# Head pairs on halves of the matmul array, and the 32-blocks of a delta rule's inverse computed on GpSimd

## The chip, the core and the metric

One core of a Trainium2 chip. The metric is the device time of one launch in microseconds. The kernel before took 853.67 us (median of 3 runs, 853.37 to 853.96). In the profile PE is the matmul engine TensorE, PEld its weight loads, DVE VectorE, ACT ScalarE, POOL GpSimd and SP SyncE, whose queue carries the weight loads from memory.

## The reference, cut to what matters

Two transformer-like blocks on 256 positions of width 1024, all float32. The first block has a state-space mixer (SSM, 16 heads of 64 columns, which the kernel computes as one causal 256 x 256 product per head), a gated linear recurrence, two gates and a feed-forward part. The second block has four branches of width 512: a gated delta rule (4 heads), a spatial gating, a sliding-window attention (8 query heads of 64, 2 key heads) and an attention over a memory (4 heads), each gated, projected up and summed.

The delta rule needs, for each chunk, the solution of a unit lower triangular system:

```
L = where(strict, (kb @ k^T) * exp(diff), 0)
sol = triangular_solve(eye + L, rhs, lower, unit_diagonal)
u, w = sol[..., :dv], sol[..., dv:]
v_new = u - w @ S;  o = qg @ S + a_qk @ v_new;  S = S * d + kd^T @ v_new
```

The reference works in chunks of 64; the kernel uses two chunks of 128 for each of 4 heads, which is the same function. So there are eight matrices of 128 x 128 to invert.

## The kernel before

The projections make up most of the work. Each weight chunk of 256 columns (or 512) is loaded by SP's queue as two tiles `wraw` of 128 x 1024, split by ACT (`whi`, L112) and DVE (`wlo`, L113) into two rounded parts, and multiplied with the activations `HH` and `HL` in three float32r matmuls per 128 rows (`mm3`, L397 to L399). A float32 matmul that is not of this kind appears as two instructions in the trace.

The order of PE's instructions is the order in which the program is written (`tc.manual_schedule` for the tensor engine). The class `Weave` writes it: the main generator (`block1`, then `block2`) emits projections and yields once after every 12 matmuls of 256 columns or 6 of 512, which is one tick. Side generators do the rest of the work; a side yields a number of ticks to wait or an event and ticks after it, and at each tick at most two sides (in block 2) take a step, in the order in which they were added: `decay`, `delta`, `memory`, `window`, `spatial`. When the main generator yields a side's name, that side is run to its end at that point (a join). The other engines' instructions are ordered by the framework.

The SSM side (`side_ssd`) makes for each head a decayed 256 x 256 matrix `M` and multiplies it with that head's 64 columns (`head`, L656 and L658). The columns stand in `XD`, for each head a 128-wide tile of which the other 64 columns are zero, so that two heads of a pair are added up into one bank `py`.

The window side (`side_window`) has for each of 8 heads a step of scores (a mask, L1326, and two products with the keys, L1327 and L1329), a step of transposes (`turn`, L1358) and a step of values (L1370, L1372). The heads of a pair lie on the two halves of the partitions; `SK` and `SV` hold keys and values with the other half zero, so that each product runs over the whole array.

The delta side (`side_delta`) computes `LT` (the transpose of L, L1144), then the inverse by doubling: level 0 on DVE (L1155, L1156) and a transpose (`pi`, L1161), then levels 1 to 6. A level l merges blocks of 2^l into blocks of 2^(l+1): a product `pit` (L1177) of 64 columns per head, a multiplication by a mask (L1180), from level 2 on a transpose `piy` of the inverse so far (L1187), a product `pix` (L1197) and an addition (L1204). Level 6 works on 64 x 64 quarters (L1199). Then come the solves (`pvn`), the state after the first chunk (`pS`) and the outputs (`po`, `pr1`, `pq1`). The steps of a level are one tick apart, those after it two.

In `block2` the projections come in the order dn (the delta rule's q, k, v), xq, sq, skv, gv, gu, z; then the delta side is joined, and for each branch n in the order 3, 2, 1, 0 come its gates (`g2`) and its projection up. The delta rule's output is branch 0.

Of the kernel before, what the change touches and what calls it, by code (L numbers as in the profile page):

```python
# [8 lines left out]
F32 = mybir.dt.float32  # L9
# [5 lines left out]
P = 128  # L15
S = 256
# [164 lines left out]
def two_blocks_kernel(  # L181
# [32 lines left out]
    pm = ctx.enter_context(tc.tile_pool(name="pm", bufs=4, space=bass.MemoryType.PSUM))  # L214

# [401 lines left out]
    XD = [big.tile([P, 8, 2, P], F32, tag=("b1", "b4")[tt], name=f"XD{tt}") for tt in range(2)]  # L617

    def side_ssd():

        for tt in range(2):
            nc.gpsimd.memset(XD[tt], 0.0)
        yield ("bc", 9)
        for g in range(2):
            pb = bank(f"pcb{g}")
            Bg = BC[:, g, :]
            Cg = BC[:, 2 + g, :]
            nc.tensor.matmul(pb[:, 128:384], Bg[:, 0:128], Cg, start=True, stop=True)
# [6 lines left out]
        pys = {}  # L635

        def decay(h):
            pe = bank(f"pe{h}")
            nc.tensor.matmul(pe[:, 0:384], sel16[:, h : h + 1].to_broadcast([P, P]), csT,
                             start=True, stop=False)  # L640
            nc.tensor.matmul(pe[:, 0:256], identr, low2r, start=False, stop=True)
            M = tmp(f"M{h}", 384, tag="pt", bufs=4)
            nc.scalar.activation(
                M[:, 0:128], pe[:, 0:128], AF.Exp, bias=ncs[:, 16 + h : 17 + h])
            nc.scalar.activation(M[:, 128:256], pe[:, 128:256], AF.Exp, bias=ncs[:, h : h + 1])
            nc.scalar.activation(M[:, 256:384], pe[:, 256:384], AF.Exp, bias=ncb[:, h : h + 1])
            nc.vector.tensor_tensor(out=M, in0=M, in1=CB[:, h // 8, :], op=ALU.mult)
            Ms[h] = M

        def head(h):  # L650
            t, j = divmod(h, 2)
            if j == 0:
                pys[t] = bank(f"py{t}")
            M = Ms.pop(h)
            o = pys[t]
            nc.tensor.matmul(o[:, 0:256], XD[0][:, t, j, :], M[:, 128:384],  # L656
                             start=j == 0, stop=False)
            nc.tensor.matmul(o[:, 128:256], XD[1][:, t, j, :], M[:, 0:128],  # L658
                             start=False, stop=j == 1)
            if j == 1:  # L660
                py = pys.pop(t)
                nc.vector.scalar_tensor_tensor(
                    XS[:, t, :], in0=XS[:, t, :], scalar=col("ssm_d", t), in1=py[:, 0:S],
                    op0=ALU.mult, op1=ALU.add)

        for h in range(-4, 18):
            if h < 0:
                p = h + 4
                yield (f"xs{p}", 7)

                pt = bank(f"pxt{p}")
                for tt in range(2):
                    for i in range(2):
                        nc.tensor.transpose(
                            pt[:, tt * S + i * P : tt * S + (i + 1) * P],
                            XS[:, 2 * p + i, tt * P : (tt + 1) * P], ident)
                for tt in range(2):
                    for j in range(2):
                        nc.vector.tensor_tensor(
                            out=XD[tt][:, 2 * p : 2 * p + 2, j, 64 * j : 64 * j + 64],  # L680
                            in0=pt[:, tt * S : (tt + 1) * S].rearrange(
                                "p (t j d) -> p t j d", j=2, d=64)[:, :, j, :],
                            in1=dt[:, tt, 4 * p + j : 4 * p + 4 : 2].unsqueeze(2).to_broadcast(
                                [P, 2, 64]),
                            op=ALU.mult)
                if p == 3:
                    yield ("z", 1)
                continue
            if h < 16:
                decay(h)  # L690
            if h >= 2:
                head(h - 2)
            yield 1
        wv.event("ssd")
# [306 lines left out]
    def block2(HH, HL, MK, MV):  # L1001
# [28 lines left out]


        SVT = bM[:, 1024:1280]
        SK = [bM[:, 1280:1536], lws[:, 9:11, :].rearrange("p a c -> p (a c)")]
        SV = bM[:, 1536:2048].rearrange("p (j t c) -> p j t c", j=2, t=2)
# [56 lines left out]
        sqs = {}  # L1091

        def side_delta():
# [60 lines left out]
            for c in range(2):  # L1154
                nc.vector.tensor_tensor(out=YI[c], in0=LT[c], in1=per4(lv0), op=ALU.mult)  # L1155
                nc.vector.tensor_tensor(out=YI[c], in0=YI[c], in1=per4(ident), op=ALU.add)  # L1156
                yield 1
            for c in range(2):
                px = bank(f"pi{c}")
                for h in range(4):  # L1160
                    nc.tensor.transpose(px[:, h * P : (h + 1) * P], YI[c][:, h, :], ident)  # L1161
                nc.scalar.copy(XI[c], v4(px))
                yield 1
# [8 lines left out]
            for l in range(1, 7):  # L1172
                for c in range(2):
# [10 lines left out]
                    if l > 1:  # L1184
                        py = bank(f"piy{l}{c}")
                        for h in range(4):
                            nc.tensor.transpose(py[:, h * P : (h + 1) * P], XI[c][:, h, :],  # L1187
                                                ident)
                        nc.scalar.copy(YI[c], v4(py))
                    yield 1  # L1190
                for c in range(2):
# [17 lines left out]
                    yield 1  # L1209
# [19 lines left out]
            yield 2  # L1229
# [12 lines left out]
            yield 2  # L1242
# [13 lines left out]
            yield 2  # L1256
            solve(1)
            yield 2
# [47 lines left out]
        def side_window():  # L1306
            nc.gpsimd.memset(SK[0][64:128], 0.0)
            nc.gpsimd.memset(SK[1][0:64], 0.0)
            nc.gpsimd.memset(SV, 0.0)
            yield ("skv", 2)  # L1310
            pv = bank("psv")
            for tt in range(2):
                nc.tensor.transpose(pv[:, tt * P : (tt + 1) * P],
                                    SVT[:, tt * P : (tt + 1) * P], ident)
            for j in range(2):
                c = slice(64 * j, 64 * j + 64)
                nc.scalar.copy(SV[:, j, :, c],
                               pv[:, 0:S].rearrange("p (t c) -> p t c", t=2)[:, :, c])
            yield 1
            heads = [t + 4 * j for t in range(4) for j in range(2)]  # L1320
            PBs, PTs, pos = {}, {}, {}

            def scores(hd):
                j, t = divmod(hd, 4)
                ps = bank(f"psc{hd}")
                nc.tensor.matmul(ps[:, 0:384], identr, swmr, start=True, stop=False)  # L1326
                nc.tensor.matmul(ps[:, 0:128], SQ[:, t, 0:P], SK[j][:, 0:P],  # L1327
                                 start=False, stop=False)
                nc.tensor.matmul(ps[:, 128:384], SQ[:, t, P:S], SK[j],  # L1329
                                 start=False, stop=True)  # L1330
# [45 lines left out]

            for i in range(10):
                if i < 8:
                    scores(heads[i])
                    yield 1  # L1380
                if 1 <= i < 9:
                    turn(heads[i - 1])
                if i >= 2:
                    values(heads[i - 2])
                yield 2
# [61 lines left out]
        def side_branch(n, ev):  # L1447
# [3 lines left out]
            y = big.tile([P, 2, 4, S], F32R, tag="b4" if n in (3, 1) else "b5", name=f"yhl{n}")  # L1451
# [55 lines left out]
        for j in range(2):  # L1507
# [25 lines left out]
        yield "decay"  # L1533
        yield "delta"
        wv.event("delta")
        wv.add("y3", side_branch(3, "memory"))
        MG = big.tile([P, 2, D], F32, tag="b3", name="MG2")
        order = (3, 2, 1, 0)
        for n in order:
# [8 lines left out]
            if n == 3:  # L1548
                yield "memory"
# [195 lines left out]
```

## Time and profile before

| | before |
|---|---|
| time, median of 3 runs | 853.67 us |
| profiled execution | 853.3 us |
| its span | 851.4 us |
| PE busy | 837.6 us, 98% |
| DVE, ACT, POOL busy | 71%, 61%, 1% |
| granted clock of PE | 1.00, mean of the span |

The span runs from the first to the last instruction on the chip; the time has some 2 us more around it. PE's matmuls are pipelined: the duration of one includes its way through the array, and the distance between two starts says what one costs in a row of them. In a row of matmuls on PE that keeps the engine full, work that is added or taken away shows in the span; on the other engines only where PE waits for them.

### The profile page before, as it was taken

To read this page: it belongs to the slowest core of one execution; us is meant where nothing else is said; L and a number is where in the kernel's file an instruction comes from. 1 tells how busy PE (TensorE), PEld (TensorE's weight loads), DVE (VectorE), ACT (ScalarE), POOL (GpSimd) and SP (SyncE) were. 2 spreads that over 40 slices of the span, in tenths; PEclk is the share of its full clock that TensorE was granted. 3 is DMA by queue.
4 is the path that set the end of the run, shared out by engine and by line. 5 is a ranking of instruction groups with operands and counts; after the bars stand their busy time and mean duration, and the time that the engine had idled before them with its cause. 6 is when DMAs were issued, how large, how long until landed. Compare 5 with 4: busy or idle time off the path is not lost.

```text
span 851.4 us, 14278 instructions
## 1 busy us (share of the span) xinstructions
PE 837.6 (98%) x5624; PEld 775.1 (91%) x5624; DVE 602.3 (71%) x1001; ACT 519.3 (61%) x790; POOL 6.8 (1%) x18
## 2 busy tenths in 40 slices
PE   6999999999999999999999999999999999999997
PEld 6999999888889999999889899999999998888886
DVE  8796874996778888888654878754557645566673
ACT  7686668884656665565543677754866754444452
POOL 2000000000000000000000000000000000000000
PEclk9999999999999999999999999999999999999999
DMA  6645343556754655555655563423322455655561
GB/s 248 237 163 197 100 140 134 202 189 208 245 175 155 213 178 194 177 177 192 216 187 180 168 205 136 149 99 100 100 73 77 156 191 196 197 195 187 185 202 50
DMA packets 39810, 144.16 MB, mean 169 GB/s; under 512 B 4416, under 2 KB 4672, under 8 KB 39488
## 3 DMA queue, kind: packets, MB, share of 16 engines
q1 hardware_dynamic: 39600, 142.73, 49.8%
q8 instruction: 44, 0.72, 0.3%
q10 hardware_dynamic: 144, 0.52, 0.2%
q14 instruction: 22, 0.18, 0.1%
HBM read 142.19 MB, written 1.05 MB: 168 GB/s over the span
## 4 chain that ended last, share of the span: by engine, by line
PE 98%; DVE 1%; DMA 1%; ACT 0%; issue 0%; DVEq 0%
PE fu L399 5%; PE fu L398 5%; PE fu L397 5%; PE g L397 5%; PE g L398 5%; PE g L399 5%; PE z L397 3%; PE z L398 3%; PE z L399 3%; PE fd L397 3%; PE fd L399 3%; PE fd L398 3%; PE up L398 2%; PE up L399 2%; PE up L397 2%; PE o L399 2%
## 5 line engine op out<-in xcount | busy, mean ns | idle before, releaser
L113 DVE TENSOR_TENSOR wlo<-wraw,whi 128x1024 fp32r<-128x1024 f32 x258 | 313.8, 1222 | 155.6 <-ACT whi L112 153.7
L112 ACT CAST whi<-wraw 128x1024 fp32r<-128x1024 f32 x258 | 269.2, 1050 | 228.2 <-PE fu L398 48.6
L397 PE MATMUL fu<-HH,whi 128*128 128x256 f32 x384 | 108.7, 283 | 0.0
L398 PE MATMUL fu<-HL,whi 128*128 128x256 f32 x384 | 108.7, 283 | 0.0
L399 PE MATMUL fu<-HH,wlo 128*128 128x256 f32 x384 | 108.7, 283 | 0.0
L397 PE MATMUL g<-whi,HH 128*128 128x512 f32 x192 | 75.7, 394 | 0.0
L399 PE MATMUL g<-whi,HL 128*128 128x512 f32 x192 | 74.8, 389 | 0.0
L398 PE MATMUL g<-wlo,HH 128*128 128x512 f32 x192 | 74.7, 389 | 0.0
L397 PEld LDWEIGHTS fu<-HH,whi 128*128 128x128 f32 x384 | 73.7, 192 | 0.0
L398 PEld LDWEIGHTS fu<-HL,whi 128*128 128x128 f32 x384 | 73.7, 192 | 0.0
L399 PEld LDWEIGHTS fu<-HH,wlo 128*128 128x128 f32 x384 | 73.7, 192 | 0.0
L397 PE MATMUL z<-HH,whi 128*128 128x256 f32 x192 | 56.2, 293 | 0.0
L399 PE MATMUL z<-HH,wlo 128*128 128x256 f32 x192 | 54.3, 283 | 0.0
L398 PE MATMUL z<-HL,whi 128*128 128x256 f32 x192 | 54.3, 283 | 0.0
L559 DVE SCALAR_TENSOR_TENSOR fc<-fu,pc,fc 128x255 f32<-128x255 f32 (+1 forms) x96 | 43.7, 478 | 1.6
L399 PEld LDWEIGHTS g<-whi,HL 128*128 128x128 f32 x192 | 36.0, 188 | 7.6
L397 PEld LDWEIGHTS g<-whi,HH 128*128 128x128 f32 x192 | 36.1, 188 | 7.4
L398 PEld LDWEIGHTS g<-wlo,HH 128*128 128x128 f32 x192 | 36.1, 188 | 7.3
L398 PE MATMUL fd<-wlo,FH 128*128 128x512 f32 (+1 forms) x120 | 41.7, 347 | 0.0
L397 PE MATMUL fd<-whi,FH 128*128 128x512 f32 (+1 forms) x120 | 41.6, 347 | 0.0
L399 PE MATMUL fd<-whi,FL 128*128 128x512 f32 (+1 forms) x120 | 41.6, 347 | 0.0
L398 PEld LDWEIGHTS z<-HL,whi 128*128 128x128 f32 x192 | 36.8, 192 | 0.1
(534 smaller groups left out, 2073.8 us busy)
## 6 DMA issues: line engine op xcount, KB each, us to landing
wraw<-in_w_in_dram SPq DMA_DIRECT2D x130, 512.0 KB, 3.5
wraw<-in_w_fu_dram SPq DMA_DIRECT2D x48, 512.0 KB, 3.7
wraw<-in_w_fd_dram SPq DMA_DIRECT2D x24, 512.0 KB, 3.9
wraw<-in_w_o_dram SPq DMA_DIRECT2D x16, 512.0 KB, 3.8
wraw<-in_w_up_dram SPq DMA_DIRECT2D x16, 512.0 KB, 3.5
wraw<-in_w_pa_dram SPq DMA_DIRECT2D x8, 512.0 KB, 4.3
wraw<-in_w_pb_dram SPq DMA_DIRECT2D x8, 512.0 KB, 4.3
wraw<-in_w_mk_dram SPq DMA_DIRECT2D x4, 512.0 KB, 4.1
```

What stands on the lines that cost most here:

```text
L112: nc.scalar.copy(hi, raw)
L113: nc.vector.tensor_tensor(out=lo, in0=raw, in1=hi.bitcast(F32), op=ALU.subtract)
L397: nc.tensor.matmul(o, wh, xh, start=first, stop=False)
L398: nc.tensor.matmul(o, wh, xl, start=False, stop=False)
L399: nc.tensor.matmul(o, wl, xh, start=False, stop=last)
L559: nc.vector.scalar_tensor_tensor(o[:, d:S], in0=p[:, 0 : S - d], scalar=col(wname, (taps - 1 - d) * n + i), in1=o[:, d:S], op0=ALU.mult, o ...
```

## The change

1. SSM: `XD` holds the 64 columns of each head without zeros. The two heads of a pair write to the two halves of the partitions of `py`, each with a 64-column weight. The products of a pair stand one behind the other in one step (`heads`).
2. Window: keys and values are kept in `SKV` and `SV` without zeros. The scores of a pair read the two halves of the partitions (64 rows each) into two banks; the values of a pair write to the two halves. The steps of the side are per pair and further apart.
3. Delta rule: levels 0 to 4 go from PE, DVE and ACT. In their place `diagonal` inverts the 32 diagonal blocks of 32 x 32 (8 matrices of 4 blocks) on GpSimd, by forward substitution of 31 steps with two operations each. The blocks go out to memory and back in, so that each of 128 partitions holds one block and 8 of the 32 columns of its inverse, and the results go out and back in again: four waves of four transfers, all issued from GpSimd. The side waits 30 ticks behind that, then does levels 5 and 6. Its steps are 2 ticks apart in the levels and 4 after them.
4. The join of the delta side moves from ahead of the first gates to behind them; some tiles change their places.

```diff
-    XD = [big.tile([P, 8, 2, P], F32, tag=("b1", "b4")[tt], name=f"XD{tt}") for tt in range(2)]
+    XD = big.tile([P, 2, D], F32, tag="b1", name="XD")
...
-        for tt in range(2):
-            nc.gpsimd.memset(XD[tt], 0.0)
...
-        def head(h):
-            t, j = divmod(h, 2)
-            if j == 0:
-                pys[t] = bank(f"py{t}")
-            M = Ms.pop(h)
-            o = pys[t]
-            nc.tensor.matmul(o[:, 0:256], XD[0][:, t, j, :], M[:, 128:384],
-                             start=j == 0, stop=False)
-            nc.tensor.matmul(o[:, 128:256], XD[1][:, t, j, :], M[:, 0:128],
-                             start=False, stop=j == 1)
-            if j == 1:
-                py = pys.pop(t)
-                nc.vector.scalar_tensor_tensor(
-                    XS[:, t, :], in0=XS[:, t, :], scalar=col("ssm_d", t), in1=py[:, 0:S],
-                    op0=ALU.mult, op1=ALU.add)
+        def heads(t):
+
+            py = bank(f"py{t}")
+            Mh = [Ms.pop(2 * t + j) for j in range(2)]
+            for tt in range(2):
+                for j in range(2):
+                    c = slice(64 * (2 * t + j), 64 * (2 * t + j) + 64)
+                    nc.tensor.matmul(
+                        py[64 * j : 64 * j + 64, P * tt : S], XD[:, tt, c],
+                        Mh[j][:, 128:384] if tt == 0 else Mh[j][:, 0:128],
+                        start=tt == 0, stop=tt == 1)
+            nc.vector.scalar_tensor_tensor(
+                XS[:, t, :], in0=XS[:, t, :], scalar=col("ssm_d", t), in1=py[:, 0:S],
+                op0=ALU.mult, op1=ALU.add)
...
-                    for j in range(2):
-                        nc.vector.tensor_tensor(
-                            out=XD[tt][:, 2 * p : 2 * p + 2, j, 64 * j : 64 * j + 64],
-                            in0=pt[:, tt * S : (tt + 1) * S].rearrange(
-                                "p (t j d) -> p t j d", j=2, d=64)[:, :, j, :],
-                            in1=dt[:, tt, 4 * p + j : 4 * p + 4 : 2].unsqueeze(2).to_broadcast(
-                                [P, 2, 64]),
-                            op=ALU.mult)
+                    nc.vector.tensor_tensor(
+                        out=XD[:, tt, p * S : (p + 1) * S].rearrange("p (h d) -> p h d", d=64),
+                        in0=pt[:, tt * S : (tt + 1) * S].rearrange("p (h d) -> p h d", d=64),
+                        in1=dt[:, tt, 4 * p : 4 * p + 4].unsqueeze(2).to_broadcast([P, 4, 64]),
+                        op=ALU.mult)
...
-            if h >= 2:
-                head(h - 2)
+            if h >= 2 and h % 2 == 1:
+                heads((h - 3) // 2)
...
-        SVT = bM[:, 1024:1280]
-        SK = [bM[:, 1280:1536], lws[:, 9:11, :].rearrange("p a c -> p (a c)")]
-        SV = bM[:, 1536:2048].rearrange("p (j t c) -> p j t c", j=2, t=2)
+        SKV = v2(bM[:, 1024:1536])
+        SV = v2(bM[:, 1536:1792])
...
+        def diagonal():
+
+            LA8 = bLA[:, 0:2].rearrange("p c h l -> p (c h) l")
+            XI8 = bXY[:, 0:2].rearrange("p c h l -> p (c h) l")
+            dl = dp.tile([8, 4, 32, 32], F32, name="dl")
+            dx = dp.tile([8, 4, 32, 32], F32, name="dx")
+
+            lb = bXY[:, 2:4].rearrange("p a h (b l) -> p (a h b) l", l=32)
+            xb = bM[:, 0:256].rearrange("p (i k) -> p i k", k=8)
+            ta = bM[:, 256:512].rearrange("p (i k) -> p i k", k=8)
+            eng = nc.gpsimd
+            for b in range(4):
+                r = slice(32 * b, 32 * b + 32)
+                eng.dma_start(dl[:, b].rearrange("c s l -> s c l"), LA8[r, :, r])
+            eng.memset(XI8, 0.0)
+            eng.memset(xb, 0.0)
+            for g in range(4):
+                q = slice(32 * g, 32 * g + 32)
+                eng.affine_select(out=xb[q], in_=xb[q], compare_op=ALU.not_equal, fill=1.0,
+                                  base=-8 * g, pattern=[[1, 32], [-1, 8]],
+                                  channel_multiplier=0)
+                eng.dma_start(lb[q], dl.rearrange("c b s l -> (c b) s l"))
+            for j in range(31):
+                n = 31 - j
+                t = ta[:, 0:n, :]
+                eng.tensor_tensor(
+                    out=t, in0=xb[:, j : j + 1, :].to_broadcast([P, n, 8]),
+                    in1=lb[:, j, j + 1 : 32].unsqueeze(2).to_broadcast([P, n, 8]),
+                    op=ALU.mult)
+                eng.tensor_tensor(out=xb[:, j + 1 : 32, :], in0=xb[:, j + 1 : 32, :], in1=t,
+                                  op=ALU.subtract)
+            for g in range(4):
+                eng.dma_start(
+                    dx[:, :, :, 8 * g : 8 * g + 8].rearrange("c b i k -> (c b) i k"),
+                    xb[32 * g : 32 * g + 32])
+            for b in range(4):
+                r = slice(32 * b, 32 * b + 32)
+                eng.dma_start(XI8[r, :, r], dx[:, b].rearrange("c i k -> i c k"))
...
-            for c in range(2):
-                nc.vector.tensor_tensor(out=YI[c], in0=LT[c], in1=per4(lv0), op=ALU.mult)
-                nc.vector.tensor_tensor(out=YI[c], in0=YI[c], in1=per4(ident), op=ALU.add)
-                yield 1
-            for c in range(2):
-                px = bank(f"pi{c}")
-                for h in range(4):
-                    nc.tensor.transpose(px[:, h * P : (h + 1) * P], YI[c][:, h, :], ident)
-                nc.scalar.copy(XI[c], v4(px))
-                yield 1
+
+            diagonal()
+            yield 30
...
-            for l in range(1, 7):
+            for l in range(5, 7):
...
-                    if l > 1:
-                        py = bank(f"piy{l}{c}")
-                        for h in range(4):
-                            nc.tensor.transpose(py[:, h * P : (h + 1) * P], XI[c][:, h, :],
-                                                ident)
-                        nc.scalar.copy(YI[c], v4(py))
-                    yield 1
+                    py = bank(f"piy{l}{c}")
+                    for h in range(4):
+                        nc.tensor.transpose(py[:, h * P : (h + 1) * P], XI[c][:, h, :], ident)
+                    nc.scalar.copy(YI[c], v4(py))
+                    yield 2
...
-                    yield 1
+                    yield 2
...
-            yield 2
+            yield 4
...
-            heads = [t + 4 * j for t in range(4) for j in range(2)]
-            PBs, PTs, pos = {}, {}, {}
-
-            def scores(hd):
-                j, t = divmod(hd, 4)
-                ps = bank(f"psc{hd}")
-                nc.tensor.matmul(ps[:, 0:384], identr, swmr, start=True, stop=False)
-                nc.tensor.matmul(ps[:, 0:128], SQ[:, t, 0:P], SK[j][:, 0:P],
-                                 start=False, stop=False)
-                nc.tensor.matmul(ps[:, 128:384], SQ[:, t, P:S], SK[j],
-                                 start=False, stop=True)
+            PBs, PTs = {}, {}
+
+            def scores(t):
+
+                two = [bank(f"psc{t + 4 * j}") for j in range(2)]
+                for ps in two:
+                    nc.tensor.matmul(ps[:, 0:384], identr, swmr, start=True, stop=False)
+                for q, c, w in ((0, 0, P), (P, P, S)):
+                    for j, ps in enumerate(two):
+                        r = slice(64 * j, 64 * j + 64)
+                        nc.tensor.matmul(ps[:, c : c + w], SQ[r, t, q : q + P], SKV[r, 0, 0:w],
+                                         start=False, stop=q == P)
+                for j, ps in enumerate(two):
+                    soft(t + 4 * j, ps)
+
+            def soft(hd, ps):
...
-            def values(hd):
-                j, t = divmod(hd, 4)
-                if j == 0:
-                    pos[t] = bank(f"pso{t}")
-                po = pos[t]
-                PT = PTs.pop(hd)
-                nc.tensor.matmul(po[:, 0:256], SV[:, j, 0, :], PT[:, 0:256],
-                                 start=j == 0, stop=False)
-                nc.tensor.matmul(po[:, 128:256], SV[:, j, 1, :], PT[:, 256:384],
-                                 start=False, stop=j == 1)
-                if j == 1:
-                    nc.vector.tensor_copy(SQ[:, t, :], pos.pop(t)[:, 0:S])
-
-            for i in range(10):
-                if i < 8:
-                    scores(heads[i])
+            def values(t):
+                po = bank(f"pso{t}")
+                PT = [PTs.pop(t + 4 * j) for j in range(2)]
+                for tt in range(2):
+                    for j in range(2):
+                        nc.tensor.matmul(
+                            po[64 * j : 64 * j + 64, P * tt : S], SV[:, tt, 64 * j : 64 * j + 64],
+                            PT[j][:, 0:256] if tt == 0 else PT[j][:, 256:384],
+                            start=tt == 0, stop=tt == 1)
+                nc.vector.tensor_copy(SQ[:, t, :], po[:, 0:S])
+
+            for t in range(5):
+                if t < 4:
+                    scores(t)
+                    yield 2
+                if t >= 1:
+                    values(t - 1)
+                yield 4
+                if t < 4:
+                    turn(t)
                     yield 1
-                if 1 <= i < 9:
-                    turn(heads[i - 1])
-                if i >= 2:
-                    values(heads[i - 2])
-                yield 2
+                    turn(t + 4)
+                    yield 3
...
-            y = big.tile([P, 2, 4, S], F32R, tag="b4" if n in (3, 1) else "b5", name=f"yhl{n}")
+            y = big.tile([P, 2, 4, S], F32R, tag=("b4", "b5", "lw")[n - 1],
+                         name=f"yhl{n}")
...
-        for j in range(2):
-            r = slice(64 * j, 64 * j + 64)
-            nc.scalar.copy(SK[j][r], b[r, 0, :])
-        nc.scalar.copy(SVT, b[:, 1, :])
+        nc.scalar.copy(SKV, b)
...
-        yield "decay"
-        yield "delta"
-        wv.event("delta")
         wv.add("y3", side_branch(3, "memory"))
-        MG = big.tile([P, 2, D], F32, tag="b3", name="MG2")
...
             if n == 3:
+                yield "decay"
+                yield "delta"
+                MG = big.tile([P, 2, D], F32, tag="b3", name="MG2")
```

Left out above: the other yields between the solves and outputs go from 2 to 4 as well, the memsets of `SK` and `SV` go, and the pool `dp`, which holds `dl` and `dx`, is in device memory. The part of `scores` behind the products stays as it was, under the name `soft`.

## Rows read from the trace of the kernel before

**Rows 1.** The page, part 1: busy time, share of the span, instructions.

```profile
PE 837.6 (98%) x5624; PEld 775.1 (91%) x5624; DVE 602.3 (71%) x1001; ACT 519.3 (61%) x790; POOL 6.8 (1%) x18
```

**Rows 2.** Waits of PE: engine, line, waited for: us in total, times, longest.

```profile
PE n_t L487 <- DVE h L477: 7.8, 1, 7.8
PE xbc L398 <- DVE HL L497: 0.2, 1, 0.2
```

**Rows 3.** Stretches: busy us and instructions of each engine, clock, DMA share, GB/s.

```profile
550.00:600.00 50.00, 50.00 (x364) 47.09 (x363) 27.15 (x60) 25.80 (x56) 0.00 (x0) 1.00 0.27 93
600.00:650.00 50.00, 50.00 (x415) 48.25 (x415) 30.39 (x80) 34.47 (x68) 0.00 (x0) 1.00 0.26 88
```

**Rows 4.** Timeline of PE from 586: start, us, engine, line, operation, tiles, count.

```profile
588.37 1.00 PE L1177 MATMUL pit<-bXY,bLA 128*128 128x64 f32 x8
589.20 0.61 PE L1187 MATMUL piy<-ident,bXY 128*128 128x128 f32 x4
589.56 0.42 PE L1326 MATMUL psc<-swmr,ident2r 128*128 128x384 f32 x1
589.82 0.38 PE L1327 MATMUL psc<-bM,bGS 128*128 128x128 f32 x2
...
591.87 1.00 PE L1197 MATMUL pix<-T,bXY 128*128 128x64 f32 x8
592.68 0.48 PE L397 MATMUL gv<-whi,HH 128*128 128x512 f32 x1
593.00 0.39 PE L398 MATMUL gv<-wlo,HH 128*128 128x512 f32 x1
593.23 0.39 PE L399 MATMUL gv<-whi,HL 128*128 128x512 f32 x1
```

**Rows 5.** Timeline of PE from 76, one SSM head and projections behind it.

```profile
80.10 0.59 PE L656 MATMUL py<-M,XD 128*128 128x256 f32 x2
80.53 0.39 PE L658 MATMUL py<-M,XD 128*128 128x128 f32 x2
80.67 0.36 PE L397 MATMUL lx<-HH,whi 128*128 128x256 f32 x1
80.87 0.28 PE L398 MATMUL lx<-HL,whi 128*128 128x256 f32 x1
80.99 0.28 PE L399 MATMUL lx<-HH,wlo 128*128 128x256 f32 x1
```

**Rows 6.** PE by line and shape: count, busy us, mean ns.

```profile
L656 PE MATMUL py<-M,XD 128*128 128x256 f32 x32 | 9.5, 378 | 0.0
```

**Rows 7.** Timeline of PE from 620, level 6 on quarters of the array.

```profile
620.44 0.68 PE L1177 MATMUL pit<-bXY,bLA 64*64 64x64 f32 x8
621.04 0.66 PE L1187 MATMUL piy<-ident,bXY 128*128 128x128 f32 x4
621.63 0.55 PE L1358 MATMUL pst<-ident,PB 128*128 128x128 f32 x3
```

**Rows 8.** Timeline of DVE from 551, the last write of `LT`.

```profile
551.79 0.34 DVE L1144 SCALAR_TENSOR_TENSOR bLA<-pkk,wk,bLA 128x128 f32<-128x128 f32 x1
```

**Rows 9.** POOL by line: count, busy us, mean ns.

```profile
L294 POOL TENSOR_SCALAR_AFFINE_SELECT triu<-one 128x128 f32<-128x128 f32 x1 | 0.3, 292 | 0.0
...
L292 POOL MEMSET one<- 128x128 f32 x1 | 0.2, 204 | 0.0
```

**Rows 10.** DVE by line from 552 to 612: count, busy us, mean ns.

```profile
L113 DVE TENSOR_TENSOR wlo<-wraw,whi 128x1024 fp32r<-128x1024 f32 x11 | 13.4, 1217 | 0.3 <-ACT whi L112 0.3
```

**Rows 11.** DMA issues: tile, queue, count, KB each, us to landing.

```profile
out_dram<-X SPq DMA_DIRECT2D x4, 256.0 KB, 2.0
...
lws<-in_lvl_dram SPq DMA_DIRECT2D x1, 288.0 KB, 4.1
...
lws<-in_wsT_dram SPq DMA_DIRECT2D x1, 256.0 KB, 3.7
...
wsmall<-in_wsm_dram SPq DMA_DIRECT2D x1, 96.0 KB, 6.4
```

More of the change, by code (lines that the diff above doesn't have):

```diff
@@ L214, in two_blocks_kernel @@
     pm = ctx.enter_context(tc.tile_pool(name="pm", bufs=4, space=bass.MemoryType.PSUM))
+    dp = ctx.enter_context(tc.tile_pool(name="dp", bufs=1, space=bass.MemoryType.DRAM))
     def bank(name):
@@ L634, in side_ssd @@
         Ms = {}
-        pys = {}
         def decay(h):
@@ L1255, in side_delta @@
             nc.vector.tensor_tensor(out=QE, in0=v4(pq1), in1=bc4(e1), op=ALU.mult)
-            yield 2
+            yield 4
             solve(1)
-            yield 2
+            yield 4
             po = bank("po1")
@@ L1306, in side_window @@
         def side_window():
-            nc.gpsimd.memset(SK[0][64:128], 0.0)
-            nc.gpsimd.memset(SK[1][0:64], 0.0)
-            nc.gpsimd.memset(SV, 0.0)
             yield ("skv", 2)
@@ L1313, in side_window @@
                 nc.tensor.transpose(pv[:, tt * P : (tt + 1) * P],
-                                    SVT[:, tt * P : (tt + 1) * P], ident)
-            for j in range(2):
-                c = slice(64 * j, 64 * j + 64)
-                nc.scalar.copy(SV[:, j, :, c],
-                               pv[:, 0:S].rearrange("p (t c) -> p t c", t=2)[:, :, c])
-            yield 1
-            heads = [t + 4 * j for t in range(4) for j in range(2)]
-            PBs, PTs, pos = {}, {}, {}
-            def scores(hd):
-                j, t = divmod(hd, 4)
-                ps = bank(f"psc{hd}")
-                nc.tensor.matmul(ps[:, 0:384], identr, swmr, start=True, stop=False)
-                nc.tensor.matmul(ps[:, 0:128], SQ[:, t, 0:P], SK[j][:, 0:P],
-                                 start=False, stop=False)
-                nc.tensor.matmul(ps[:, 128:384], SQ[:, t, P:S], SK[j],
-                                 start=False, stop=True)
+                                    SKV[:, 1, tt * P : (tt + 1) * P], ident)
+            nc.scalar.copy(SV, pv[:, 0:S].rearrange("p (t c) -> p t c", t=2))
+            yield 1
+            PBs, PTs = {}, {}
[11 more added lines that the diff above has]
+            def soft(hd, ps):
                 mx = sm.tile([P, 2], F32, tag="smx", name=f"smx{hd}")
@@ L1362, in turn @@
                 PTs[hd] = PT
-            def values(hd):
-                j, t = divmod(hd, 4)
-                if j == 0:
-                    pos[t] = bank(f"pso{t}")
-                po = pos[t]
-                PT = PTs.pop(hd)
-                nc.tensor.matmul(po[:, 0:256], SV[:, j, 0, :], PT[:, 0:256],
-                                 start=j == 0, stop=False)
-                nc.tensor.matmul(po[:, 128:256], SV[:, j, 1, :], PT[:, 256:384],
-                                 start=False, stop=j == 1)
-                if j == 1:
-                    nc.vector.tensor_copy(SQ[:, t, :], pos.pop(t)[:, 0:S])
-            for i in range(10):
-                if i < 8:
-                    scores(heads[i])
-                    yield 1
-                if 1 <= i < 9:
-                    turn(heads[i - 1])
-                if i >= 2:
-                    values(heads[i - 2])
-                yield 2
+            def values(t):
[14 more added lines that the diff above has]
+                    values(t - 1)
+                yield 4
+                if t < 4:
+                    turn(t)
+                    yield 1
+                    turn(t + 4)
+                    yield 3
             wv.event("window")
@@ L1506, in block2 @@
         _, b = yield from proj_fm("skv", HH, HL)
-        for j in range(2):
-            r = slice(64 * j, 64 * j + 64)
-            nc.scalar.copy(SK[j][r], b[r, 0, :])
-        nc.scalar.copy(SVT, b[:, 1, :])
+        nc.scalar.copy(SKV, b)
         wv.event("skv")
```

## The prediction

> **What bounds the kernel now.** I read the shares of the page first: the matmul engine (PE) is busy for 98% of the span, DVE 71%, GpSimd (POOL) 1% [rows 1]. Then the waits of PE: one of 7.8 us at the start, before the first transposes, and next to nothing after it [rows 2]. Then the stretches in which the change lies: from 550 to 650 us PE is busy in every microsecond, at the full granted clock, while DVE and ACT stand at 51 to 69% [rows 3]. PE's order is written out by hand, so the end comes when PE has worked through its list: a microsecond taken from the list is a microsecond of time, and a microsecond in which PE waits at the head of its list is one lost. Everything below is therefore either PE work or a PE wait. The profiled execution took 853.3 us (span 851.4, 1.9 around it), against a median of 853.67; the sum starts from 853.3.
>
> **The inversion on PE, levels 0 to 4 removed.** I price by the distance between starts, since durations overlap in the pipeline. Four `pit` products take 589.20 - 588.37 = 0.83 us, four transposes `piy` 589.56 - 589.20 = 0.36, four `pix` products 592.68 - 591.87 = 0.81 [rows 4]. Removed are, each for two chunks: `pi` (2 x 0.36 = 0.72), `pit` of four levels (8 x 0.83 = 6.64), `pix` of four levels (8 x 0.81 = 6.48) and `piy` of levels 2 to 4 (6 x 0.36 = 2.16): 16.0 us. Behind such an insert the first matmul of the projection lasts longer: 592.68 to 593.00 is 0.32, the next is 0.23, so 0.09 each; 18 inserts go, 1.6 us. Together **-17.6 us**. Levels 5 and 6, the solves and the products after them stay, further apart in the list but no longer.
>
> **Head pairs on halves.** Before, one SSM head takes 0.43 us for the 256-wide product and 0.22 for the 128-wide (80.10 to 80.53; 80.53 to 80.67 and 0.08 by which the next projection matmul is late) [rows 5]: 0.65, and 1.30 for a pair. The number of products stays, each on half of the array. One float32 product is two instructions (32 for 16 calls [rows 6]). Window scores and window values have the same widths: 8 pairs of SSM heads, 4 of scores, 4 of values, so 16 x 1.30 = 20.8 us of such work. No row shows two products on different halves at once. If they don't overlap, nothing is saved; if wholly, 10.4 us. I take a value between: the two instructions of one product follow one another on one half, so in the order a a b b (wide, 0.215 each) c c d d (narrow, 0.11 each) the second of a product can lie beside the first of the next, and no more: 3 x 0.215 + 2 x 0.11 = 0.86 a pair in place of 1.30. With 0.43 saved, 16 x 0.43 = **-6.9 us**. Changing between whole array and part is not free: the four level-6 products on 64 x 64 are followed by four transposes that take 621.63 - 621.04 = 0.59 in place of 0.36 [rows 7], 0.23 more. I take 0.2 a group, 16 groups: **+3.2 us** (bounds 0 and 16 x 0.23 = 3.7). The Trainium skill, page "TensorEngine Tiling (Array Packing)", Key Properties, says that changing the tiling mode drains the engine, while different tiles run in parallel. By that rule the trace agrees in the first half (0.23 us), and no row here shows the second. By that page's "up to 2x" the pairs alone would give the 10.4 us of the bound.
>
> **What goes away off the path.** 16 scalings into `XD` become 8 wider ones, the zeroing of `XD`, `SK` and `SV` on POOL goes, and DVE and ACT lose the multiplications and copies of four levels. None of it is what PE waits for [rows 2], so I cost it at nothing.
>
> **The new chain on POOL, and the one new wait.** It starts when the last `LT` is written, 551.79 + 0.34 = 552.1 us [rows 8]. PE's next step of the branch, `pit` of level 5, comes 30 ticks after the `diagonal` step. A tick is 12 projection matmuls of 0.12 us [rows 5] or 6 wide ones of 0.235 [rows 4], 1.42 us: 30 x 1.42 = 42.6. Beside them the memory branch (three scores and four values of 0.86, four transposes of 0.36: 7.5) and half of the window branch (two score pairs 2 x (2 x 0.26 + 0.86), twelve transposes of 0.09, a value pair 0.86: 4.8) and some 14 inserts of 0.09 (1.2): 56 us. So POOL has from 552.1 to about 607, **55 us**. All other work behind the `pit` in PE's list, projections included, waits with it if POOL is late, since the list is in order; DVE, ACT and the weight loads then fill their buffers and stop.
>
> What POOL must do: 62 operations whose mean size is 8 x 16 = 128 elements a partition. No row shows a two-input operation of POOL; the nearest are its 128x128 memset at 204 ns and its 128x128 select at 292 ns [rows 9]. By these 12.6 or 18.1 us; I take 18.1. From above, each of them may also sit out a DVE operation of the longest common sort, 1217 ns [rows 10]: 62 x 1.51 = 94. DVE spends 13.4 of 60 us in these [rows 10], a quarter, and half of one is 0.6 us, so 62 x 0.25 x 0.6 = 9 us is what I add. Then 16 transfers in four waves, each wave needing the one before (out, in, out, in). Small transfers of SP's queue land after 2.0 to 4.1 us, and 6.4 in the crowd at the start [rows 11]; four waves at 4.1 are 16.4 (8 to 25.6); strictly one behind the other, 16 x 3.7 = 59. POOL's own transfers have no row. They go by POOL's queue, behind its own operations; in this block nothing else stands in that queue, and SP's queue of weight loads is not touched, only the engines beneath, 27% busy here [rows 3]. Memsets and selects on the side, eight or so, 2.5 us. Sum: 18.1 + 9 + 16.4 + 2.5 = 46 us, under 55 by 9; ends 12.6 + 8 = 21 and 94 + 59 = 153. I take 46, thus no wait, with little to spare. The Trainium skill, "GPSIMD Engine Reference", section 3.1, gives a two-input float32 operation of 2048 elements as 4497 ns; an estimate by that page, 7936 elements at 2.2 ns, is 17.4 us before any fixed part; no run here shows it. By that the sum would be some 6 us longer if each operation has a fixed part of 0.1 us, 52, and POOL still hidden.
>
> **The join.** Counted by the yields from the block's first tick, the branch's last step moves from tick 71 to tick 97, the join from 92 to 108. So the join finds it finished, as before, and the delta output is needed only ahead of the last gates' products. If POOL is late, the whole list shifts and the join still costs nothing.
>
> **Sum.** 853.3 - 17.6 - 6.9 + 3.2 = **832 us**, POOL hidden.
>
> **Rivals.** (a) POOL is late, but by less than what is saved. The chain takes between 55 and 76 us, for instance because transfers of pieces of 32 to 128 bytes land later than 4.1 us, or DVE's two-input operations and POOL's hold each other up more often. For it: the spare 9 us is less than the doubt in any of the three terms. Against: two terms are already taken high, the landing at the slower end of its rows and a DVE surcharge that no row shows. At a chain of 65 PE waits 10: 842. The Trainium skill, "SBUF — State Buffer", says that a DVE operation with two SBUF inputs and a GpSimd operation that reads SBUF exclude one another for the whole instruction; the trace before has no such meeting to show it.
> (b) Slower than before: the chain passes 55 + 21.3 = 76 us, and PE stands at the level-5 `pit` for longer than all that was saved. Its price is one for one from there. Transfers that go strictly one behind the other, 59, with 18.1 and 2.5, make 80, which is already past it; with the 9 for DVE 89, a wait of 34: 866. For it: nothing in the trace shows POOL issuing a transfer, and four of the transfers cut their data in 1024 pieces of 32 bytes. Against: by the code a transfer waits only for the wave before its own, not for its neighbours.
> (c) Halves don't run side by side: 853.3 - 17.6 + 3.2 = 839, POOL hidden. For it: no row shows overlap.
> (d) Savings and wait cancel within 0.2% (1.7 us, about what a measurement of this kernel tells from no change): 853.
>
> **Chances.** Forecast 0.40; (a) 0.25; (b) 0.17; (c) 0.15; (d) 0.03. Faster by over 0.2%: 0.40 + 0.25 + 0.15 = 0.80; within: 0.03; slower: 0.17. The forecast's own range is 825 (whole overlap, changes of tiling free) to 839. The range reaches to 862, which takes in (a), (c), (d) and the near third of (b), and down to 824, leaving about 0.15 out.
>
> **What the profile after would show.** Right: no wait of PE on `pit`; the last `dx` load landing before PE reaches level 5; the projection of the first gates starting some 20 us earlier; `py`, `psc` and `pso` pairs in about 0.86 us. Wrong: a wait of PE ended by a POOL transfer or operation (then its length is the step that failed), pairs at 1.3 us, or DVE's weight splits growing past 1.22 us so that projections wait for `wlo`.

## The result, and the profile after

The changed kernel takes **844.29 us** (median of 4 runs, 843.45 to 845.6) against 853.67: ratio 0.9892, 95% interval 0.9874 to 0.9909. That is 9.4 us faster where 21.7 were forecast. The profiled execution took 844.04 us (span 842.3, mean granted clock 0.993).

The page, part 1, as in [rows 1], and the chain that ended last:

```profile
PE 819.2 (97%) x5464; PEld 749.4 (89%) x5464; DVE 593.8 (70%) x973; ACT 511.9 (61%) x777; POOL 53.4 (6%) x97
...
PE 89%; POOL 5%; DMA 2%; DVE 2%; issue 1%; ACT 1%; DVEq 0%; POOLq 0%
```

PE has 18.4 us less to do than in [rows 1], and yet the time fell by half of that. POOL and its transfers are on the chain now, with 5% and 2% of the span. The waits of PE, as in [rows 2], say where:

```profile
PE pit L1200 <- DMA bXY<-dx: 8.7, 1, 8.7
PE n_t L488 <- DVE h L478: 8.0, 1, 8.0
...
```

The wait at the start stayed (7.8 and 8.0). The first `pit` of level 5 waits 8.7 us for the last wave of transfers that POOL issues. The stretches of [rows 3], and small ones around the wait (same columns):

```profile
550.00:600.00 50.00, 50.00 (x352) 45.52 (x352) 34.43 (x74) 34.60 (x73) 38.18 (x62) 1.00 0.47 141
600.00:650.00 50.00, 41.26 (x325) 38.46 (x324) 24.14 (x50) 23.81 (x39) 8.64 (x17) 0.90 0.35 102
...
608.00:610.00 2.00, 0.00 (x0) 0.00 (x0) 0.00 (x0) 0.00 (x0) 0.00 (x0) 1.00 0.97 315
610.00:612.00 2.00, 0.00 (x0) 0.00 (x0) 0.00 (x0) 0.00 (x0) 0.30 (x1) 0.93 0.35 143
612.00:614.00 2.00, 0.00 (x0) 0.00 (x0) 0.00 (x0) 0.00 (x0) 2.00 (x4) 0.50 0.16 33
...
616.00:618.00 2.00, 2.00 (x11) 2.00 (x11) 0.42 (x1) 0.04 (x1) 0.00 (x0) 0.50 0.00 0
...
620.00:622.00 2.00, 2.00 (x11) 1.56 (x11) 0.00 (x0) 0.00 (x0) 0.00 (x0) 0.52 0.00 0
622.00:624.00 2.00, 2.00 (x19) 1.67 (x19) 1.16 (x5) 0.00 (x0) 0.00 (x0) 1.00 0.00 0
```

PE stops at 606.4, and from 608 DVE and ACT stand still too, as the prediction argued from full buffers. The granted clock is at its upper level (2.4 GHz) until 610, falls during 610 to 612 to the lower one (0.50, 1.2 GHz), and is still there when PE works again, until just before 622. In 616 to 618 PE finishes 11 instructions, in 622 to 624 it finishes 19. The timeline of PE, first at a pair of SSM heads (to be held against [rows 5]), then around the wait:

```profile
81.89 0.28 PE L639 MATMUL pe<-low2r,ident2r 128*128 128x256 f32 x1
82.09 0.87 PE L655 MATMUL py<-M,XD 128*64 128x256 f32 x8
82.89 0.39 PE L398 MATMUL lx<-HH,whi 128*128 128x256 f32 x1
83.11 0.28 PE L399 MATMUL lx<-HL,whi 128*128 128x256 f32 x1
...
606.14 0.28 PE L400 MATMUL z<-HH,wlo 128*128 128x256 f32 x1
615.09 1.94 PE L1200 MATMUL pit<-bXY,bLA 128*128 128x64 f32 x8 [8.67 <-DMA bXY<-dx]
...
618.74 0.41 PE L399 MATMUL z<-HL,whi 128*128 128x256 f32 x1
618.95 0.41 PE L400 MATMUL z<-HH,wlo 128*128 128x256 f32 x1
...
623.52 0.28 PE L400 MATMUL z<-HH,wlo 128*128 128x256 f32 x1
623.64 0.28 PE L398 MATMUL z<-HH,whi 128*128 128x256 f32 x1
```

The pair's eight instructions take 82.89 - 82.09 = 0.80 us, and the changes of tiling 0.20 - 0.12 ahead of it and 0.22 - 0.12 behind it, 0.18: 0.98 in place of 1.30. After the wait the same projection matmul follows the one before it after 0.21 us, later after 0.12. From 615.09 to 621.9 PE works at half clock. Work whose spacing doubles would lose half of these 6.8 us, 3.4; at the projections' spacing it is 6.8 x (1 - 0.12 / 0.21) = 2.9; so some 3 us. 844.04 - 8.67 - 3 = 832.4, close to the forecast sum: what was missed lies in the wait and the clock behind it, if nothing else is wrong in two places that cancel. The runs below test that.

The chain on POOL in its timeline (a transfer's row is the time that POOL spends issuing; four each):

```profile
550.29 2.47 POOL L1097 DMA_DIRECT2D dl<-bLA  x4 [62.30 <-DVE XPB L1431]
554.65 2.10 POOL L1105 DMA_DIRECT2D bXY<-dl  x4 [1.89 <-DMA dl<-bLA]
562.24 0.61 POOL L1109 TENSOR_TENSOR bM<-bM,bXY 128x248 f32<-128x248 f32 x1 [5.49 <-DMA bXY<-dl]
562.93 0.72 POOL L1113 TENSOR_TENSOR bM<-bM 128x248 f32<-128x248 f32 x1
...
569.51 1.41 POOL L1109 TENSOR_TENSOR bM<-bM,bXY 128x208 f32<-128x208 f32 x1
571.00 1.50 POOL L1113 TENSOR_TENSOR bM<-bM 128x208 f32<-128x208 f32 x1
...
603.35 0.20 POOL L1109 TENSOR_TENSOR bM<-bM,bXY 128x8 f32<-128x8 f32 x1
603.63 0.20 POOL L1113 TENSOR_TENSOR bM<-bM 128x8 f32<-128x8 f32 x1
604.13 3.11 POOL L1116 DMA_DIRECT2D dx<-bM  x4 [0.29 <-POOL bM L1113]
611.70 2.33 POOL L1121 DMA_DIRECT2D bXY<-dx  x4 [4.47 <-DMA dx<-bM]
```

It runs from 550.29 to 615.09, 64.8 us. Two waves take 562.24 - 550.29 = 11.95, the 62 operations 603.83 - 562.24 = 41.6, the other two waves 615.09 - 603.83 = 11.3. Issuing alone holds POOL for 2.47 + 2.10 + 3.11 + 2.33 = 10.0 us of the waves' 23.2.

Beside the operations of 1.4 and 1.5 us stands this row of DVE's timeline (two weight splits, 1.45 us each where [rows 10] has 1.22):

```profile
569.10 2.89 DVE L113 TENSOR_TENSOR wlo<-wraw,whi 128x1024 fp32r<-128x1024 f32 x2
```

### The profile page after: what moved, and what is told of

Its sections match the earlier page's. It is cut to its first block, busy times and chain, and to the rows that moved or that the text cites. A ratio compares the mean times of both kernels' runs of the same rounds, so it can differ in the third digit from the quotient of the medians.

```text
span 842.3 us, 14020 instructions
## 1 busy us (share of the span) xinstructions
PE 819.2 (97%) x5464; PEld 749.4 (89%) x5464; DVE 593.8 (70%) x973; ACT 511.9 (61%) x777; POOL 53.4 (6%) x97
## 4 chain that ended last, share of the span: by engine, by line
PE 89%; POOL 5%; DMA 2%; DVE 2%; issue 1%; ACT 1%; DVEq 0%; POOLq 0%
PE fu L399 5%; PE fu L398 5%; PE fu L400 5%; PE g L398 5%; PE g L399 5%; PE g L400 5%; PE z L398 3%; PE fd L398 3%; PE fd L399 3%; PE fd L400 3%; PE z L399 2%; PE z L400 2%; POOL bM L1113 2%; POOL bM L1109 2%; PE up L399 2%; PE up L398 2%
## 5 line engine op out<-in xcount | busy, mean ns | idle before, releaser
L398 PE MATMUL fd<-whi,FH 128*128 128x512 f32 (+1 forms) x120 | 41.6, 347 | 0.0
L400 PE MATMUL fd<-whi,FL 128*128 128x512 f32 (+1 forms) x120 | 41.6, 347 | 0.0
L398 PEld LDWEIGHTS z<-HH,whi 128*128 128x128 f32 x192 | 37.2, 194 | 0.8 <-issue 0.7
```

The lines of the kernel that those rows point to most:

```text
L398: nc.tensor.matmul(o, wh, xh, start=first, stop=False)
L400: nc.tensor.matmul(o, wl, xh, start=False, stop=last)
```

## The experiments

The theory, A in the expectations: the sum for PE was right, and the chain on POOL is longer than the work that PE has beside it. The rivals say that the parts were worth less or hinder each other in another place, or that the chain is long for another reason. Runs of before on the same chips took 853.74 to 853.89 us.

**Later.** The changed kernel with ten more ticks ahead of level 5.

```diff
             diagonal()
-            yield 30
+            yield 40
```

> The changed kernel with 40 ticks in place of 30 between the GpSimd chain and level 5. Theory A (POOL's chain is 65 us long and PE comes to level 5 after 56; the wait of 8.7 us and the half clock after it, some 3 us, are all that is missing): PE comes ten ticks, 14 us, and the window's work between later, near 622 us, the chain ends at 615, no wait, no fall of the clock: 844.3 - 8.7 - 3.2 = 832. Rival B (the PE work saved is itself smaller, or a later branch runs into the join at tick 108): the wait goes but another comes, at the last steps of the branch or at the join: 836 to 844.

Measured: **832.45 us** (832.18 to 832.63), ratio to before 0.975 (0.9735 to 0.9764). Its waits of PE, and PE in the second stretch:

```profile
PE n_t L488 <- DVE h L478: 8.4, 1, 8.4
PE mv L399 <- DVE wlo L113: 0.2, 1, 0.2
PE pcT L368 <- DVE pcT_cat L322: 0.2, 1, 0.2
...
600.00:650.00 50.00, 50.00 (x426) 47.54 (x426) 30.86 (x63) 33.37 (x57) 9.13 (x18) 1.00 0.47 142
```

The wait is gone, the clock stays at 1.00, and the branch still finishes before its join. 21.4 us are saved where the sum had 21.3. The first `pit` starts at 626.2, 4 us later than expected; POOL has issued its last transfer by 614.5. Of all versions that leave nothing out this one is the fastest.

**Sooner.** Ten ticks fewer.

```diff
             diagonal()
-            yield 30
+            yield 20
```

> The changed kernel with 20 ticks in place of 30. Theory A (a wait of PE is paid one for one and in addition a fixed sum for the clock): PE comes to level 5 some 16 us sooner, at 590, the chain ends near 613 (somewhat sooner, since DVE is idle while PE waits): a wait of 23 us, 832 + 23 + 3 = 858, slower than before. Rival B (the wait is partly made up, by the weights that are split in the meantime): no more than 850.

Measured: 854.87 us (854.43 to 856.24, 10 runs), ratio 1.0014 (1.0005 to 1.0023): all that was saved is gone. Its wait, stretches within and behind it, and POOL's third wave:

```profile
PE pit L1200 <- DMA bXY<-dx: 19.9, 1, 19.9
...
598.00:600.00 2.00, 0.00 (x0) 0.00 (x0) 0.00 (x0) 0.00 (x0) 1.53 (x7) 0.50 0.00 0
...
610.00:612.00 2.00, 2.00 (x12) 2.00 (x11) 0.53 (x2) 0.00 (x0) 0.00 (x0) 0.50 0.00 0
...
616.00:618.00 2.00, 2.00 (x20) 2.00 (x19) 2.00 (x7) 1.41 (x2) 0.00 (x0) 1.00 0.21 27
...
600.31 3.10 POOL L1116 DMA_DIRECT2D dx<-bM  x4 [0.29 <-POOL bM L1113]
```

832.45 + 19.9 = 852.3. Behind the wait PE works at half clock from 609.5 to 614.0, of which some 2 us are lost by the working above: 854.3, where this execution took 854.51. The wait costs one for one. The expectation was 3 us too high: with DVE stopped as well, POOL is no longer held up and issues its third wave at 600.3 instead of 604.1, and that wave lands 1.7 us faster.

**Without DVE's two-input operations in the stretch.** In weight halves 180 to 191 the low part is set to zero, so their low-part products are left out of the result.

```diff
-            nc.vector.tensor_tensor(out=lo, in0=raw, in1=hi.bitcast(F32), op=ALU.subtract)
+            if 180 <= j < 192:
+                nc.vector.memset(lo.bitcast(F32), 0.0)
+            else:
+                nc.vector.tensor_tensor(out=lo, in0=raw, in1=hi.bitcast(F32), op=ALU.subtract)
```

> The changed kernel, where for the twelve weight halves of the stretch of POOL's chain DVE's subtraction (two SBUF inputs) is replaced by a memset of the low part, so these low parts are left out of the products. Theory A (13 of POOL's 62 operations last 0.8 us longer because DVE's two-input operation stands in their way): POOL's 62 operations take 32 to 33 us in place of 41.6, the chain ends near 606, PE waits 0 to 1 us: 832 to 834. Rival B (POOL's operations are just uneven, DVE has no part): 41 us and the same wait, 844.

Measured: 834.47 us, ratio 0.9766 (0.9739 to 0.9793). The median lies between runs of 832.1, 832.7, 836.3 and 836.7 us; the trace is of the one at 836.3. From it: the wait, POOL by line, POOL's timeline.

```profile
PE pit L1204 <- DMA bXY<-dx: 2.2, 1, 2.2
...
L1117 POOL TENSOR_TENSOR bM<-bM 128x248 f32<-128x248 f32 (+30 forms) x31 | 14.4, 465 | 2.4
L1113 POOL TENSOR_TENSOR bM<-bM,bXY 128x248 f32<-128x248 f32 (+30 forms) x31 | 13.8, 445 | 7.8 <-DMA bXY<-dl 5.5
...
562.48 0.61 POOL L1113 TENSOR_TENSOR bM<-bM,bXY 128x248 f32<-128x248 f32 x1 [5.46 <-DMA bXY<-dl]
595.74 3.11 POOL L1120 DMA_DIRECT2D dx<-bM  x4 [0.29 <-POOL bM L1117]
604.52 2.33 POOL L1125 DMA_DIRECT2D bXY<-dx  x4 [5.67 <-DMA dx<-bM]
```

The 62 operations take 595.45 - 562.48 = 33.0 us, so DVE cost them 41.6 - 33.0 = 8.6; the forecast had 9. But 33.0 is 0.53 each with no weight split in the way, not 0.292. The third wave, issued 8.4 us sooner, took 1.2 longer to land, and PE still waits 2.2 us in this execution. The Trainium skill, "SBUF — State Buffer", section "SBUF: two separate sides", says that a DVE operation with two SBUF inputs and a GpSimd operation that reads SBUF shut one another out; by that rule the trace agrees, with 8.6 us over 62 operations.

**The steps on DVE.** The 62 operations on the other vector engine.

```diff
-                eng.tensor_tensor(
+                nc.vector.tensor_tensor(
                     out=t, ...
-                eng.tensor_tensor(out=xb[:, j + 1 : 32, :], in0=xb[:, j + 1 : 32, :], in1=t,
+                nc.vector.tensor_tensor(out=xb[:, j + 1 : 32, :], in0=xb[:, j + 1 : 32, :], in1=t,
```

> The changed kernel with 30 ticks, where DVE and not POOL does the 62 operations of the substitution; the transfers stay on POOL. Theory A (the step that failed is the 0.53 us that one POOL operation takes without DVE in its way; DVE's of 128 elements takes 0.28 in the scalings into XD): 17 us and DVE's other work between them, some 30 us in place of 41.6, the chain ends near 604, no wait on level 5: 832 to 835. Rival B (DVE's queue is what the projections live on there; the steps push the weight splits and the softmax back): PE waits for wlo or for the window's steps instead, 836 to 845.

Measured: 835.97 us (834.2 to 838.2), ratio 0.9792 (0.9773 to 0.9811). The wait, and one of the two groups of DVE by line:

```profile
PE pit L1200 <- DMA bXY<-dx: 1.4, 1, 1.4
...
L1109 DVE TENSOR_TENSOR bM<-bM,bXY 128x248 f32<-128x248 f32 (+30 forms) x31 | 8.9, 288 | 0.5
```

An operation of this chain is 288 ns on DVE and 445 on POOL undisturbed. Yet DVE has its own work between, so the third wave is issued at 595.82, no sooner than in the run before. PE waited no longer for the weight splits than in the 40-tick kernel (0.2 us), and not for the window. The time is a little over the 832 to 835 expected; of the 3.5 us above the 40-tick kernel the wait explains 1.4, and the rest is not settled.

**Pairs alone.** The kernel before with the pairs of the SSM and the window on halves, and its inversion as it was.

```diff
-            diagonal()
-            yield 30
+            for c in range(2):
+                nc.vector.tensor_tensor(out=YI[c], in0=LT[c], in1=per4(lv0), op=ALU.mult)
...
-            for l in range(5, 7):
+            for l in range(1, 7):
```

> The kernel before with the head pairs on halves alone (SSM and window), the inversion on PE as before. If a pair costs what the changed kernel's trace shows (0.80 us and 0.18 of change of tiling, against 1.30), 16 groups save 16 x 0.32 = 5 us: 848.5. If the halves gave nothing and all of the gain is the inversion: 853.7 or somewhat above. As predicted (0.86 and 0.2): 850.

Measured: 849.18 us (848.81 to 849.3), ratio 0.9945 (0.993 to 0.996): the pairs are worth 4.7 us. The sum had 6.9 - 3.2 = 3.7. At 0.98 a pair, 16 x 0.32 would be 5.1; but the last SSM pair takes 1.17 us in this run (113.03 to 114.20) and not 0.80, which leaves 4.7.

**Both heads on the same half.** The 40-tick kernel, with the two heads of an SSM pair on the same 64 output partitions, one after the other. Only the lower 64 channels are updated; the upper half is left out.

```diff
-            for tt in range(2):
-                for j in range(2):
+            for j in range(2):
+                for tt in range(2):
...
-                        py[64 * j : 64 * j + 64, P * tt : S], XD[:, tt, c],
+                        py[0:64, S * j + P * tt : S * j + S], XD[:, tt, c],
```

> The changed kernel with 40 ticks, where the products of both SSM heads of a pair go to the same half of the array, into different columns of the bank; the update leaves out the upper half of the channels. Theory A (two halves work side by side; that is what makes a pair 0.80 us): 8 pairs go to about 1.3 us, 4 us more than the 832.5 of the version with 40 ticks: 836.5. Rival B (a pair is cheaper because its weights are 64 columns wide, whichever half): no change, 832.5.

Measured: 836.7 us (836.63 to 837.49), ratio 0.9801 (0.9787 to 0.9816), 4.25 over the 40-tick kernel. A pair in PE's timeline:

```profile
87.37 1.51 PE L655 MATMUL py<-M,XD 128*64 128x256 f32 x8
88.81 0.39 PE L398 MATMUL lx<-HH,whi 128*128 128x256 f32 x1
```

1.44 us on one half, 0.80 on two: the halves do work side by side, which rival (c) denied. Eight SSM pairs at 0.64 would be 5.1; but the last pair on two halves takes 1.17 in the 40-tick kernel too, so it is 7 x 0.64 + 0.28 = 4.8. Of this 4.25 show in the time, since in the traced execution the first pair came 0.6 us sooner than in that of the 40-tick kernel (82.29 and 82.86). The Trainium skill, "TensorEngine Tiling (Array Packing)", Key Properties, has different tiles run in parallel; by that rule this run agrees, as no row before could show.

**Inversion alone.** The kernel before with the inversion on POOL, 40 ticks and the join behind the first gates, and the SSM and window as they were.

```diff
-            for l in range(1, 7):
+            diagonal()
+            yield 40
+            for l in range(5, 7):
```

> The kernel before with the inversion of the blocks on GpSimd and 40 ticks behind it, without the head pairs. Theory A (the two parts add up): the pairs alone saved 4.7 us, the two together with 40 ticks 21.4, so the inversion alone 16.7: 837. My sum had 17.6: 836. Rival B (the parts help one another, for instance because the window's unpaired steps fill the place behind the chain or DVE is fuller): 839 or more, or 835 or less.

Measured: 843.68 us (843.32 to 845.09), ratio 0.9879 (0.9863 to 0.9896), 6.7 over the expectation: a miss. Of its trace: PE's wait, ACT's timeline ahead of it, PE's timeline.

```profile
PE pst L1389 <- DVE PB L1379: 4.6, 1, 4.6
...
588.60 1.28 ACT L1373 ACT_TABLE_LOAD   x1
590.48 1.28 ACT L1546 ACT_TABLE_LOAD   x1
592.39 1.28 ACT L1375 ACT_TABLE_LOAD   x1
593.69 0.30 ACT L1375 ACTIVATE ssu<-smx,pr 128x2 f32<-128x2 f32 x1
...
594.97 0.95 PE L1389 MATMUL pst<-ident,PB 128*128 128x128 f32 x3 [4.65 <-DVE PB L1379]
```

POOL was in time; another wait took its place, and the clock stood at 0.50 behind it (596 to 600). The window's softmax (L1373, L1375) and the gates' function (L1546) now fall into the same microseconds on ACT, which loads a table of 1.28 us at each change between them, and the window's transposes come one tick behind its scores, before the softmax is done. The expectation, which took the parts to be independent, had left out that the change also moves the window's steps further apart.

**The same with the window's steps apart.** One line more:

```diff
                     scores(heads[i])
-                    yield 1
+                    yield 3
```

> The run with the inversion alone and 40 ticks, where the window's scores stand 3 ticks ahead of the step behind them in place of 1. In the run before it PE waited 4.6 us for a softmax of the window, whose activations stood in ACT's queue between four table loads of 1.28 us, and the clock halved. Theory A (the inversion alone is worth 16.7 us as a sum of PE work, and that wait hid a part of it): with four more microseconds for the softmax the wait goes: 837. Rival B (the inversion alone is worth only the 10 us that the run showed): 843 to 844 again, whatever the window's steps do.

Measured: 837.19 us (836.83 to 837.49), ratio 0.9805 (0.9789 to 0.9822), with no wait at `pst`. The inversion alone is worth 853.74 - 837.19 = 16.55 us, where the sum had 17.6. With 4.7 for the pairs that makes 21.3, against 21.4 for both together: the parts add up once their waits are gone.

## Why the prediction was wrong

- **The failed step: what POOL must do.** 46 us were forecast and 64.8 measured, against a budget of 55 that was right within 1 us (the chain starts at 550.3, forecast 552.1, and PE stops at 606.4, forecast "about 607"). The step took 18.1 for the 62 operations, from the single-input select of [rows 9] at 292 ns. Without DVE in the way they take 33.0: 455 ns each, and 77 ns between one and the next, 62 x (0.163 + 0.077) = 14.9 more. The bounds (12.6 and 94) held it; the value taken stood near the lower one, because that row was the nearest by size, and not by the kind of operation.
- **The waves.** 16.4 forecast, 23.2 measured. A wave was priced as one landing. But POOL issues its four transfers one after another, 2.1 to 3.1 us a wave, before the last of them can land: 10.0 us of issuing had no term, while the rest, 13.2, is below the 16.4. [rows 11] show SP's landings and no time of issuing. This is read from the trace; no run changed the waves alone.
- **DVE in POOL's way.** 9 forecast, 8.6 measured. The size was right in part by luck: in the trace ten operations are longer by 0.8 to 1.1 us, where the forecast had a quarter of 62 by 0.6. The selects and memsets (2.5) were off the chain. 46 + 14.9 + 6.8 - 0.4 - 2.5 = 64.8.
- **The price of being late.** 8.67 us of wait, one for one, as rival (a) and (b) had it, and some 3 us more that no case had: the clock falls while PE waits. Rival (a), "at a chain of 65 PE waits 10: 842", is what happened, with 0.25 against the forecast's 0.40. Of its reasons the later transfers hold in part, as issuing; DVE and POOL did not hold each other up more than forecast, and the largest part, the operations' own price, it did not name. "With little to spare" should have shifted weight to it, since three terms without a row stood against 9 us.
- **PE's own sum was right**: 832 forecast, 832.45 with the wait removed. That it is so close is luck: within it the inversion was 1 us too high and the saving by the pairs 1 us too low (0.98 a pair with its changes of tiling, forecast 0.86 + 0.2 = 1.06). The halves overlap, a little more than argued (0.80 for 0.86); that they do so product by product, as argued, was not tested.
- **The join and the edits priced at nothing** cost nothing in the 40-tick kernel. But the window's wider steps are not idle: the inversion-alone run without them lost 6.5 us (843.68 and 837.19). The forecast's tick count took the wider spacing for granted and never asked what it covers.

## What to carry to other kernels

Where a chain on another engine is hidden behind a fixed number of steps, work out how late it may be before any other thing becomes late, and put the slack there: ten ticks more were worth 11.8 us here and cost nothing. Price an operation that no row shows from the row nearest in kind (inputs, engine) with a fixed part for each, and a transfer as issuing plus landing. A wait of PE cost its length here and, behind the waits of 2.2 us and more in block 2, the time at half clock as well.

## What the runs showed of the hardware

- A two-input float32 operation on POOL takes 0.28 us from start to start at 8 elements a partition (603.35 to 603.63) and 0.69 for the multiplication at 248. What even the smallest takes is about half of the time in this kernel: 62 x 0.28 = 17 of the 33 us.
- POOL's transfers hold POOL for 0.5 to 0.8 us each: least in the second wave, whose rows are 4 KB by the code (2.10 us for four), most in the third, in pieces of 32 bytes (3.11). The first three waves landed 1.9 to 5.7 us after their last transfer was issued. The same third wave landed after 2.8 us with the weight loads stopped (the 20-tick kernel), and after 4.5 and 5.7 beside them.
- The granted clock fell to its lower level between 610 and 612, while PE waited, and stayed there for 6.8 us of PE's work after the wait, some 3 us lost. Behind 19.9 us of wait (the 20-tick kernel) it was 4.5 us of work. In the run without DVE's splits the clock was 0.50 from 610 to 612, behind a wait of only 2.2 us (606.7 to 608.9); in the run with the steps on DVE, with a wait of 1.4 us, it stayed at 1.00. The four runs without DVE's splits fit that price, though only one has a trace: 832.1 and 832.7 us at a mean granted clock of 0.999 and 0.998, 836.3 and 836.7 at 0.996.
